# A hybrid SSD and attention layer: the decay products of the scan on VectorE instead of GpSimd, and two sets of attention logits in one step of the plan

## The chip, the cores and the metric

One core of a Trainium2 chip runs the whole layer as one program. The metric is the device time of one execution in microseconds. Engines are named as in the profile: PE (TensorE matmuls), PEld (TensorE weight loads), DVE (VectorE), ACT (ScalarE), POOL (GpSimd), SP (SyncE, which here only issues transfers).

## The reference

One layer of a streaming encoder, for a prompt of 1024 rows and eight running streams of 16 rows each, 1152 rows together. Each row is projected to 12336 columns; two mixers run on the result, a chunked state-space scan (32 heads in 8 groups) and an attention with forget gates (16 heads), and their gated sum is projected again and normalized.

```python
h = einsum('bld,de->ble', x, w_in)
z, xbc, dt_raw, q, k, v, f_raw, g_path, mg_m, mg_a = split_projection(h)
xbc = silu(causal_conv(xbc))                       # x, B and C columns
acum  = cumsum(dt * A)                             # per chunk and head
decay = exp(where(causal, acum[:, None] - acum[None], -inf))
m      = (C @ B^T) * decay * dt
y_diag = m @ x
y_off  = (C @ state) * exp(acum)                   # per chunk, state carried on
y = rmsnorm_groups((y_diag + y_off + d_skip * x) * silu(z)) * mnorm_w
s = q @ k^T / 8 + (c_q - c_k), masked;  o = softmax(s) @ v    # c: cumsum of log f
u = sigmoid(g_m) * (y @ w_br_m) + sigmoid(g_a) * ((o * silu(g_path)) @ w_br_a)
x_new = layer_norm(2**0.25 * x + u @ w_out)
```

The streams do the same with a cached state, and with 1024 cached keys and values ahead of their own 16 rows. Everything is float32.

## The kernel before, in words

Activations lie with columns on the partitions and the 1152 rows along the free axis, in three pieces (`c` = 0, 1, 2) of 384. A dense tile (`dense`) makes 128 output columns: for each piece 8 slices of the input times three products (L244, L245, L246; weights and activations are split into a high and a low part), 24 matmuls into one PSUM bank named `d`. There are two such banks, so a piece can begin when the piece before the last has been emptied by ACT and DVE. After every six dense matmuls the program calls `flow.tick()`, which may put a step of some other work, written as a generator, between them on PE.

In the scan stage the dense tiles of group g + 1 (in the order z0, x0, x1, z1, b, c) run beside the scan of group g. A convolved tile is emptied by ACT (L539, L540, and L545 for the streams' part of the third piece), then worked on by DVE (three L551), ACT (L552) and DVE (L553). A z tile takes ACT L569 and DVE L570. Each new weight tile is split by ACT (L223 or L226, `wh`) and then by POOL (L224) or DVE (L227, `wl`).

The scan of a group goes through the pieces c = 0, 1, 2, called its three blocks below. For each block `decay` makes, for four heads: `m`, the differences of the cumulative decays (DVE, L687, three instructions per head), the exponential of `ce` in place (ACT, L689), the exponential of `m` (ACT, L690), `m` times the causal C B^T (DVE, L691), and `ce` times C (L692), which stands in the matmul with the carried state (L712). `ce` is the row of cumulative decays, loaded from DRAM onto all partitions. POOL also gates the outputs (L724), adds their squares (L730), scales x by the weights (L614) and the state by its decay (L667).

In the scan stage a scheduler orders the instructions of each engine by their due times, so taking an instruction to another engine changes the order around it. From attention on the order is the one in which the code is written, under `tc.manual_schedule()`.

Attention runs per pair of heads (`pair`), beside the dense tiles of the next pair. Its steps stand in a table `plan`: a due time, a cost that is taken off the time to the next step, and the functions to call. A step whose time has come is called at the next tick. `scores(j, i)` makes the prompt's logits of query block j against key block i in a PSUM tile `s2` (two buffers), `least` and `mins` their row minima, and `s_scores(half)` the logits of four of the eight streams against their cached keys, in another `s2` buffer and a bank `y`.

Of the kernel before, what the change touches and what calls it, by code (L numbers as in the profile page):

```python
# [15 lines left out]
ALU = mybir.AluOpType  # L16
# [133 lines left out]
def trunk_step(ctx: ExitStack, tc: tile.TileContext, I, O):  # L150
    nc = tc.nc
    ve, ac, po, te, sy = nc.vector, nc.scalar, nc.gpsimd, nc.tensor, nc.sync
# [438 lines left out]
    def group(g, r):  # L591

        sp = lazy["spb"]
        xs, z, Bf, Cf = [r["x0"], r["x1"]], [r["z0"], r["z1"]], r["b"], r["c"]
# [84 lines left out]
        def decay(c, i):  # L679
            w = CW if c < 2 else 256  # L680
            for e in range(2):
                h = 4 * g + 2 * i + e
                m = sp.tile([P, 3, P], F32, tag="m", name=f"m{c}_{h}", bufs=4)
                ce = ces[c, 2 * i + e]
                for j in range(3):
                    b = 3 * c + j
                    ve.tensor_scalar(m[:, j, :], ce[:, j * P:(j + 1) * P], nacum[:, b, h:h + 1], 0.0,  # L687
                                     ALU.add, ALU.min)
                ac.activation(ce[:, :w], ce[:, :w], AF.Exp)  # L689
                ac.activation(m[:], m[:], AF.Exp)  # L690
                ve.tensor_tensor(m[:], m[:], cbms[c][:], ALU.mult)  # L691
                po.tensor_tensor(ce[:, :w], ce[:, :w], Cf[c][:, :w], ALU.mult)  # L692
                mm[c, 2 * i + e] = m

        def readout(c):
# [76 lines left out]
        for c in range(NCH):  # L772
            for j in range(3):
                transp(3 * c + j)
                yield Y
                if c and j == 0:
                    readout(c - 1)
                    yield 2 * Y
            cbt(c)
            yield Y  # L780
            if c == 2:
                stk = stack()
                sample_out()
                yield Y
            decay(c, 0)
            yield Y
            states(c)
            if c == 2:
                for q in range(4):
                    sample_decay(q)  # L790
            yield Y
            decay(c, 1)
            if c < 2:
                for i in range(2):
                    rows(c + 1, i)
            yield Y
# [80 lines left out]
    def pair(hp, r):  # L877
# [227 lines left out]
        def last(i):  # L1105
# [32 lines left out]
            (45.7, 4.4, (values, 2), (scores, 1, 0), (scores, 1, 1), (least, 1, 0)),  # L1138
            (46.0, 0.0, (load, "v", hp, 1, 0)),
            (49.4, 0.0, (least, 1, 1), (mins, 1, 1, "a")),  # L1140
            (53.8, 0.8, (scores, 0, 0)),
            (54.6, 0.0, (least, 0, 0), (mins, 0, 0, "a")),
            (55.4, 2.6, (s_scores, 1)),
            (62.2, 0.2, (share, "a", (0, 1))),
            (62.4, 0.0, (s_weights, 1)),
            (62.8, 0.0, (load, "v", hp, 1, 1)),
# [64 lines left out]
    with tc.manual_schedule():  # L1211
        r = keys(0, r)
        for hp in range(1, 8):
            flow.start(pair(hp - 1, r))
            gate_dense(GATES_SSD + hp - 1, fp, "kv1", 3)
            r = keys(hp, q_and_gate(hp))
        flow.start(pair(7, r))
        for j in range(GATES_SSD + 7, GATES_SSD + 7 + GATES_FOX):
            gate_dense(j, fp, "kv1", 3)
        flow.drain()  # L1220
# [139 lines left out]
    for c in range(NCH):  # L1360
# [27 lines left out]
        for j in range(3):  # L1388
            b, w = 3 * c + j, width[j]
# [107 lines left out]
```

## Time and profile before

| | |
|---|---|
| median of 3 runs | 2066.13 us (2064.82 to 2066.86) |
| the profiled execution | 2064.78 us |
| its span | 2062.9 us, 36057 instructions |
| granted TensorE clock | 0.999 of full speed |
| scan with its dense tiles | about 190 to 1000 us, some 100 us per group |
| attention with its dense tiles | about 1000 to 1650 us |
| branch and output projections | the rest |

A row of the stretches view gives the stretch, its length, then busy time and number of instructions of PE, PEld, DVE, ACT and POOL, the granted clock, the share of the DMA engines and GB/s. A row of the groups view gives line, engine, operation, output and inputs, shapes and count, then busy time and mean ns of one, then the idle time of the engine ahead of them and what ended it. A row of the waits view names the waiting engine and line, what it waited for, the sum in us, how often, and the longest. A row of a timeline gives start and duration in us, the instruction, how many were merged, and in brackets the idle time of the engine ahead of it with what ended that. Matmuls are pipelined: the distance of two starts is what one costs.

### The profile page before, as it was taken

What the parts mean: (1) busy time and instruction counts of PE and PEld (TensorE: products, weight loads), DVE (VectorE), ACT (ScalarE), POOL (GpSimd) and SP (SyncE); (2) the same over time, 40 slices, a digit from 0 to 9 for tenths busy, and PEclk for the clock granted to TensorE, in tenths of its full rate; (3) what the DMA queues carried; (4) which work ended last, traced back from release to release, by engine and by line L of the source; (5) the groups of instructions that cost most, each with busy time, mean ns of one, the idle gap of its engine ahead of it and who ended that gap; (6) DMA issues with size and microseconds to landing.
All of it is one profiled execution on the core that took longest, in us unless ns stands there. A gap on an engine that the chain in (4) does not pass through costs nothing.

```text
span 2062.9 us, 36057 instructions
## 1 busy us (share of the span) xinstructions
PE 2028.5 (98%) x14263; PEld 1868.2 (91%) x14263; DVE 1376.8 (67%) x2278; ACT 820.1 (40%) x1647; POOL 594.6 (29%) x775
## 2 busy tenths in 40 slices
PE   9999999999999999999999999999999999999998
PEld 7899989899998999999988888888889899999987
DVE  4145788887878787874487787777777774173355
ACT  5124444444434344443445554545455452122210
POOL 0013565555556564644100100110010002114400
PEclk9999999999999999999999999999999999999999
DMA  6412242423232323242556566556656584154222
GB/s 221 161 65 90 71 134 71 126 77 119 81 126 78 118 91 114 87 134 91 185 196 194 186 206 207 188 179 199 212 184 202 186 301 147 41 171 152 82 106 92
DMA packets 123624, 292.49 MB, mean 142 GB/s; under 512 B 18632, under 2 KB 74944, under 8 KB 113216
## 3 DMA queue, kind: packets, MB, share of 16 engines
q1 hardware_dynamic: 110912, 208.93, 31.7%
q10 hardware_dynamic: 12544, 81.27, 11.4%
q8 instruction: 112, 1.84, 0.4%
q14 instruction: 56, 0.46, 0.1%
HBM read 233.64 MB, written 56.51 MB: 141 GB/s over the span
## 4 chain that ended last, share of the span: by engine, by line
PE 67%; DVE 20%; ACT 5%; DMA 4%; issue 2%; POOL 1%; ACTq 0%; DVEq 0%; SPq 0%; POOLq 0%
PE d L244 14%; PE d L246 13%; PE d L245 13%; PE s L914 3%; DVE m L687 2%; PE o L989 2%; PE v L333 2%; PE v L334 2%; PE v L332 2%; PE dq L245 2%; PE dq L244 2%; PE dq L246 2%; PE out L1381 2%; PE out L1380 2%; PE out L1382 2%
## 5 line engine op out<-in xcount | busy, mean ns | idle before, releaser
L244 PE MATMUL d<-xh,wh 128*128 128x384 f32 x2112 | 740.9, 351 | 21.3 <-DVE z3z L570 2.1
L246 PE MATMUL d<-xh,wl 128*128 128x384 f32 x2112 | 708.7, 336 | 0.0
L245 PE MATMUL d<-xl,wh 128*128 128x384 f32 x2112 | 707.8, 335 | 0.0
L244 PEld LDWEIGHTS d<-xh,wh 128*128 128x128 f32 x2112 | 397.2, 188 | 54.6 <-issue 17.7
L245 PEld LDWEIGHTS d<-xl,wh 128*128 128x128 f32 x2112 | 397.6, 188 | 0.8
L246 PEld LDWEIGHTS d<-xh,wl 128*128 128x128 f32 x2112 | 396.7, 188 | 0.0
L224 POOL TENSOR_TENSOR wl<-wr,wh 128x1024 fp32r<-128x1024 f32 x52 | 125.5, 2413 | 348.8 <-ACT wh L223 348.8
L687 DVE TENSOR_SCALAR m<-ce,nacum 128x128 f32<-128x128 f32 x288 | 141.6, 553 | 5.9 <-PE y L708 5.9
L223 ACT CAST wh<-wr 128x1024 fp32r<-128x1024 f32 x64 | 67.0, 1047 | 194.9 <-PE d L245 157.1
L919 ACT ACTIVATE st<-s,ckt 128x256 f32<-128x256 f32 (+1 forms) x320 | 115.1, 466 | 20.1 <-PE s L914 14.8
L923 POOL TENSOR_TENSOR st<-st,mask_bf 128x256 f32<-128x256 f32 x64 | 48.3, 775 | 196.8 <-ACT st L919 196.7
L979 ACT ACTIVATE st<-st 128x1024 f32<-128x1024 f32 x80 | 83.1, 1062 | 43.6 <-DVE st L974 41.0
L227 DVE SCALAR_TENSOR_TENSOR wl<-wr,wh 128x1024 fp32r<-128x1024 f32 x50 | 62.2, 1243 | 32.5 <-ACT wh L226 32.1
L614 POOL TENSOR_TENSOR wx<-xdt,wdt 128x256 f32<-128x256 f32 x72 | 56.8, 790 | 50.9 <-DVE xdt L612 50.9
L989 PE MATMUL o<-st,vt 128*64 128x256 f32 (+1 forms) x640 | 69.5, 363 | 1.6 <-ACT st L979 1.2
L989 PEld LDWEIGHTS o<-st,vt 128*64 128x64 f32 x640 | 42.8, 137 | 28.4 <-ACT st L979 5.1
L245 PE MATMUL d<-yb1l,wh 128*128 128x384 f32 x192 | 64.2, 334 | 0.0
L244 PE MATMUL d<-yb1h,wh 128*128 128x384 f32 x192 | 64.2, 334 | 0.0
L246 PE MATMUL d<-yb0h,wl 128*128 128x384 f32 x192 | 64.2, 334 | 0.0
L246 PE MATMUL d<-yb1h,wl 128*128 128x384 f32 x192 | 64.2, 334 | 0.0
L245 PE MATMUL d<-yb0l,wh 128*128 128x384 f32 x192 | 64.2, 334 | 0.0
L244 PE MATMUL d<-yb0h,wh 128*128 128x384 f32 x192 | 64.2, 334 | 0.0
(635 smaller groups left out, 4093.9 us busy)
## 6 DMA issues: line engine op xcount, KB each, us to landing
wr<-in_wt SPq DMA_DIRECT2D x88, 512.0 KB
kc<-in_cache_k ACTq DMA_DIRECT2D x32, 1024.0 KB
vc<-in_cache_v ACTq DMA_DIRECT2D x32, 1024.0 KB
ce<-ac_d SPq DMA_DIRECT2D x96, 192.0 KB
wr<-in_wbr SPq DMA_DIRECT2D x24, 512.0 KB
gate_d<-gate SPq DMA_DIRECT2D x48, 192.0 KB
sb<-cs_d ACTq DMA_DIRECT2D x16, 576.0 KB
yr<-ym_d SPq DMA_DIRECT2D x16, 576.0 KB
```

The source lines that it names most:

```text
L223: ac.copy(hi[:, :cols], raw[:, :cols])
L224: lazy.get("sub", po).tensor_tensor(lo[:, :cols], raw[:, :cols], hi[:, :cols].bitcast(F32), ALU.subtract)
L227: ve.scalar_tensor_tensor(lo[:, :cols], raw[:, :cols], scale, hi[:, :cols].bitcast(F32), ALU.mult, ALU.subtract)
L244: te.matmul(out, wh, xh, start=(k == 0), stop=False)
L245: te.matmul(out, wh, xl, start=False, stop=False)
L246: te.matmul(out, wl, xh, start=False, stop=(k == n - 1))
L614: po.tensor_tensor(wx[b][:], xdt[b][:], wdt[:, b, hs][:, :, None].to_broadcast([P, 4, 64]), ALU.mult)
L687: ve.tensor_scalar(m[:, j, :], ce[:, j * P:(j + 1) * P], nacum[:, b, h:h + 1], 0.0, ALU.add, ALU.min)
L914: te.matmul(ps2[:, e, 256 * x + q0:256 * x + 256], kk[hr, ks], qq[hr, qs], start=(at == 0), stop=(at == 2))
L919: ac.activation(S[j][:, e, kb, q0:], ps2[:, e, 256 * x + q0:256 * x + 256], AF.Identity, bias=ckt[:, kb, 2 * hp + e:2 * hp + e + 1])
L979: ac.activation(w, w, AF.Exp, scale=-1.0)
L989: te.matmul(o[64 * e:64 * e + 64, 256 * at + q0:256 * at + 256], vt[:, kb, 64 * e:64 * e + 64], S[j][:, e, kb, q0:256], start=(kb == 0), s ...
```

## The change

There are two edits. The product of `ce` with C is issued on DVE instead of POOL, 96 instructions in all (8 groups, 3 blocks, 4 heads). And in the plan of a head pair the block 0 logits with their minima and the streams' second logits, three steps before, are one step with the sum of their costs.

```diff
@@ decay(c, i), in the scan
                 ac.activation(ce[:, :w], ce[:, :w], AF.Exp)
                 ac.activation(m[:], m[:], AF.Exp)
                 ve.tensor_tensor(m[:], m[:], cbms[c][:], ALU.mult)
-                po.tensor_tensor(ce[:, :w], ce[:, :w], Cf[c][:, :w], ALU.mult)
+                ve.tensor_tensor(ce[:, :w], ce[:, :w], Cf[c][:, :w], ALU.mult)
                 mm[c, 2 * i + e] = m
@@ plan, in pair(hp, r)
             (49.4, 0.0, (least, 1, 1), (mins, 1, 1, "a")),
-            (53.8, 0.8, (scores, 0, 0)),
-            (54.6, 0.0, (least, 0, 0), (mins, 0, 0, "a")),
-            (55.4, 2.6, (s_scores, 1)),
+            (53.8, 3.4, (scores, 0, 0), (least, 0, 0), (mins, 0, 0, "a"), (s_scores, 1)),
             (62.2, 0.2, (share, "a", (0, 1))),
```

What the first edit does to the order is seen at the second block of a group, here the scan of group 3 (heads 12 to 15) beside the tiles `acc4x` and `raw4x` of group 4. On DVE before: the last differences `m`, three L551 on the second piece of an x tile, and what follows.

```order
L687 TENSOR_SCALAR m_14_5481<-ce_14_5190,nacum 128x128 x3
L687 TENSOR_SCALAR m_15_5489<-ce_15_5192,nacum 128x128 x3
L551 SCALAR_TENSOR_TENSOR acc4x_1_5279<-raw4x_1_5278,cw,acc4x_1_5279 128x384 x3
L553 SCALAR_TENSOR_TENSOR acc4x_1_5279<-raw4x_1_5278,acc4x_1_5279 128x384
L612 TENSOR_TENSOR xdt_4_5334<-tp_4_5330,dtm 128x256
L227 SCALAR_TENSOR_TENSOR wl_5341<-wr_5136,wh_5340 128x1024
```

DVE now, in the same place:

```order
L687 TENSOR_SCALAR m_15_5489<-ce_15_5192,nacum 128x128 x3
L551 SCALAR_TENSOR_TENSOR acc4x_1_5279<-raw4x_1_5278,cw,acc4x_1_5279 128x384
L692 TENSOR_TENSOR ce_13_5188<-ce_13_5188,acc3c_4911 128x384
L551 SCALAR_TENSOR_TENSOR acc4x_1_5279<-raw4x_1_5278,cw,acc4x_1_5279 128x384
L692 TENSOR_TENSOR ce_14_5190<-ce_14_5190,acc3c_4911 128x384
L551 SCALAR_TENSOR_TENSOR acc4x_1_5279<-raw4x_1_5278,cw,acc4x_1_5279 128x384
L692 TENSOR_TENSOR ce_15_5192<-ce_15_5192,acc3c_4911 128x384
L612 TENSOR_TENSOR xdt_4_5334<-tp_4_5330,dtm 128x256
L227 SCALAR_TENSOR_TENSOR wl_5341<-wr_5136,wh_5340 128x1024
L553 SCALAR_TENSOR_TENSOR acc4x_1_5279<-raw4x_1_5278,acc4x_1_5279 128x384
```

Three products stand between and behind the L551 (the fourth, of head 12, stands a few rows ahead), and L553 has moved behind the weight split.

ACT in the same place, as one piece of the difference (- before, + now):

```order
 L689 ACTIVATE ce_15_5192<-ce_15_5192 128x384
 L690 ACTIVATE m_15_5489<-m_15_5489 128x384
+L226 ACTIVATE wh_5340<-wr_5136 128x1024
 L552 ACTIVATE raw4x_1_5278<-acc4x_1_5279 128x384
-L226 ACTIVATE wh_5340<-wr_5136 128x1024
 L539 COPY raw4x_2_5313<-d_2_5288 128x256
 L540 ACTIVATE acc4x_2_5314<-d_2_5288,cb,cw 128x384
```

The weight split now stands ahead of the tanh L552 that needs DVE's L551, and so no longer between it and the evacuation of the third piece.

In the scan PE has the same rows in the same order as before. In attention, PE at the block 0 logits of the first pair (`s_0_0`), before:

```order
L914 MATMUL s_0_0_11034<-qh_10011,kh_10363 128x128 x2
L914 MATMUL s_0_0_11034<-ql_10012,kh_10363 128x128 x2
L914 MATMUL s_0_0_11034<-qh_10011,kl_10364 128x128 x2
L244 MATMUL d_1_11026<-xh_92,wh_10684 128x384
L245 MATMUL d_1_11026<-xl_93,wh_10684 128x384
L246 MATMUL d_1_11026<-xh_92,wl_10685 128x384
```

and now:

```order
L914 MATMUL s_0_0_11034<-qh_10011,kh_10363 128x128 x2
L914 MATMUL s_0_0_11034<-ql_10012,kh_10363 128x128 x2
L914 MATMUL s_0_0_11034<-qh_10011,kl_10364 128x128 x2
L1038 LDWEIGHTS ident_bf
L1038 MATMUL sn_1_11062<-mask_bf,ident_bf 32x128
```

The streams' second logits (`sn_1`, `ss_1`) follow at once; before, six dense matmuls stood between. It is so in all eight pairs. DVE and POOL keep their order there.

## The prediction

> **What bounds the kernel now.** I read the busy times first, then stretches of the span, then what PE waits for, then the timelines of DVE, ACT and POOL around those waits.
>
> ```profile
> PE 2028.5 (98%) x14263; PEld 1868.2 (91%) x14263; DVE 1376.8 (67%) x2278; ACT 820.1 (40%) x1647; POOL 594.6 (29%) x775
> ...
> 470.00:570.00 100.00, 96.83 (x658) 91.35 (x657) 81.58 (x150) 43.11 (x94) 57.08 (x77) 1.00 0.31 101
> ...
> 1200.00:1300.00 100.00, 100.00 (x949) 86.56 (x944) 75.61 (x105) 51.38 (x101) 11.18 (x20) 1.00 0.63 204
> ```
>
> PE is the bound at full clock (1.00). The two stretches are one scan group and a piece of attention: in the scan PE is idle 3 us in 100, in attention not at all. So edit 1 (the products) can win only PE's idle time in the scan, and edit 2 (the logits) only the cost of changing between kinds of matmul. Idle PE time over the scan (190 to 1000 us), first the group that carries it, then the waits, first and last of each kind:
>
> ```profile
> L244 PE MATMUL d<-xh,wh 128*128 128x384 f32 x1183 | 415.9, 352 | 21.3 <-DVE z3z L570 2.1 <-DVE z6z L570 1.8 <-DVE z2z L570 1.8
> ...
> PE d L244 <- DVE z3z L570: 2.1, 2, 1.6
> ...
> PE d L244 <- DVE z4z L570: 1.8, 2, 1.5
> PE d L244 <- ACT raw1x L545: 1.0, 1, 1.0
> ...
> PE d L244 <- ACT raw2x L545: 1.0, 1, 1.0
> ...
> PE d L244 <- ACT raw4c L545: 0.4, 1, 0.4
> PE d L244 <- ACT raw3c L545: 0.4, 1, 0.4
> ```
>
> Seven z waits make 2.1 + 6 x 1.8 = 12.9 us, seven x waits 7.0, two c waits 0.8: 20.7 of the 21.3. In each the next dense chunk wants a PSUM bank `d` that ACT or DVE has not emptied. The question is whether edit 1 makes the emptying earlier or later.
>
> **Edit 1: 96 products move from POOL to DVE.** First what they cost where they are: the first block of heads in one group, on DVE and POOL.
>
> ```profile
> L692 POOL TENSOR_TENSOR ce<-ce,acc3c 128x384 f32<-128x384 f32 (+1 forms) x12 | 12.0, 1009 | 9.2 <-DVE acc3c L553 5.0 <-ACT ce L689 4.2
> ...
> 494.13 1.26 DVE L687 TENSOR_SCALAR m<-ce,nacum 128x128 f32<-128x128 f32 x2
> 495.31 4.10 DVE L551 SCALAR_TENSOR_TENSOR acc3c<-raw3c,cw,acc3c 128x384 f32<-128x384 f32 x3
> ...
> 494.30 1.99 POOL L692 TENSOR_TENSOR ce<-ce,acc3c 128x384 f32<-128x384 f32 x2 [5.00 <-DVE acc3c L553]
> ...
> 497.71 1.28 POOL L692 TENSOR_TENSOR ce<-ce,acc3c 128x384 f32<-128x384 f32 x1
> ...
> 554.79 0.48 DVE L687 TENSOR_SCALAR m<-ce,nacum 128x128 f32<-128x128 f32 x2
> ...
> 540.01 0.62 DVE L551 SCALAR_TENSOR_TENSOR acc4x<-raw4x,cw,acc4x 128x384 f32<-128x384 f32 x1
> 540.54 0.55 DVE L691 TENSOR_TENSOR m<-m,cbm 128x384 f32<-128x384 f32 x1
> 541.01 0.61 DVE L551 SCALAR_TENSOR_TENSOR acc4x<-raw4x,cw,acc4x 128x384 f32<-128x384 f32 x1
> ```
>
> With POOL idle (the last four rows) two L687 take 0.48 us, an L551 takes 540.54 - 540.01 = 0.53 of DVE's time and an L691, a product of two SBUF tiles of the moved shape, 541.01 - 540.54 = 0.47. Beside L692 two L687 take 1.26 and three L551 4.10: DVE loses 0.78 + (4.10 - 1.59) = 3.3 us to four products, 0.8 each. Such DVE work gets through about once per POOL instruction.
>
> The price of one moved product is therefore bounded by the cost 0.47 less a relief up to 1.0 (a mean L692 is 1009 ns): -0.53 to +0.47 us, and up to +1.4 if it is itself caught behind a POOL product that stays (L724, L730, about 1 us each). I take -0.35 (0.47 - 0.8), since these rows show exactly this work; here it makes 4 x -0.35 = -1.4 us. A 256-wide product (third block) I take as 0.34 us, an estimate between L687 and L691 by width.
>
> The x wait, second block of heads, on DVE, POOL, ACT and PE:
>
> ```profile
> 526.13 3.79 DVE L687 TENSOR_SCALAR m<-ce,nacum 128x128 f32<-128x128 f32 x7
> 529.84 3.18 DVE L551 SCALAR_TENSOR_TENSOR acc4x<-raw4x,cw,acc4x 128x384 f32<-128x384 f32 x3
> ...
> 526.29 1.01 POOL L724 TENSOR_TENSOR z3z<-z3z,yt 128x384 f32<-128x384 f32 x1 [0.69 <-DVE yt L721]
> 527.26 1.01 POOL L692 TENSOR_TENSOR ce<-ce,acc3c 128x384 f32<-128x384 f32 x1
> 528.22 1.02 POOL L730 TENSOR_TENSOR sqs<-sqs,yt 128x384 f32<-128x384 f32 x1
> ...
> 529.97 2.63 POOL L692 TENSOR_TENSOR ce<-ce,acc3c 128x384 f32<-128x384 f32 x2 [0.56 <-ACT ce L689]
> ...
> 533.11 0.53 ACT L552 ACTIVATE raw4x<-acc4x 128x384 f32<-128x384 f32 x1 [1.98 <-DVE acc4x L551]
> 533.54 1.04 ACT L226 ACTIVATE wh<-wr 128x1024 fp32r<-128x1024 f32 x1
> 535.31 0.27 ACT L545 COPY raw4x<-d 128x128 f32<-128x128 f32 x1
> ...
> 535.62 0.45 PE L244 MATMUL d<-xh,wh 128*128 128x384 f32 x1 [1.02 <-ACT raw4x L545]
> ```
>
> PE wants the bank at 534.6 (535.62 - 1.02). Before it is free, DVE must finish three L551 (533.0), then ACT does L552, L226 (1.04) and the evacuation, ending 535.58. Relief up to there: the three L551 lose 3.18 - 1.59 = 1.6 us to two L692, the pair before them, one of which stands at 527.26, 0.8 each as above, together 3.2. The new code puts three products ahead of or between them (the fourth stands behind): 3 x 0.47 = 1.4. The L551 end about 1.8 earlier, at 531.2. In the new order ACT also does L226 ahead of L552, while DVE still works, which takes its 1.04 off the chain: the bank is free near 535.6 - 1.8 - 0.8 = 533.0, before 534.6. All of the x wait goes: -7.0 us. If the relief were absent, L226's move alone would bring it 0.8 earlier and the products 1.4 later.
>
> The z wait, third block of heads:
>
> ```profile
> 553.30 0.52 ACT L552 ACTIVATE raw4x<-acc4x 128x384 f32<-128x384 f32 x1 [3.93 <-DVE acc4x L551]
> ...
> 562.17 0.52 ACT L690 ACTIVATE m<-m 128x384 f32<-128x384 f32 x1 [0.61 <-DVE m L687]
> 562.60 0.47 ACT L569 ACTIVATE z4z<-d 128x384 f32<-128x384 f32 x1
> ...
> 558.48 3.60 DVE L687 TENSOR_SCALAR m<-ce,nacum 128x128 f32<-128x128 f32 x5
> ...
> 563.10 0.56 DVE L570 SCALAR_TENSOR_TENSOR z4z<-z4z,d 128x384 f32<-128x384 f32 x1 [0.69 <-ACT z4z L569]
> ...
> 563.71 0.44 PE L244 MATMUL d<-xh,wh 128*128 128x384 f32 x1 [1.54 <-DVE z4z L570]
> ```
>
> The z evacuation L569 is queued on ACT behind the last exponential, which waits for L687; five of them take 3.60 us instead of 5 x 0.2 + 0.1 = 1.1. L724 and L730 stay on POOL, so perhaps half of that is won back, and two products (0.7) now stand between the last L687 and L570 on DVE, each waiting for its own ACT exponential. Going through the new order by hand, the bank comes 0.7 us earlier from the same start (between 0 and 1.4). The start moves too: at 553.30 ACT had waited 3.93 us for DVE, so the chain into this block is paced by DVE and ACT, not by PE, and inherits some 2.5 us from the second block, of which PE takes back 1.0 since its x wait is gone. Together 0.7 + 1.5 = 2.2 against the 1.54 needed. Margin 0.7, error of about 1: I leave 0.35 per group, 7 x 0.35 = 2.5, and take 12.9 - 2.5 = 10.4.
>
> The c waits hang on the first block, 1.4 us earlier by the sum above: -0.8. Behind the moved products on DVE stand L551, L612 and L570, counted above; ACT's L552 and L569 wait for them. POOL loses 12.0 us per group, its products that stay come earlier; PE reads `ce` only a block later. On SP only one store and one load at the last group change places: 0.
>
> **Edit 2: the second logits follow block 0's at once.** The kernel already does one such pair adjacent (blocks of j = 2 and the first logits); rows of PE, first the adjacent, then the separated pair:
>
> ```profile
> 1103.97 0.34 PE L246 MATMUL d<-xh,wl 128*128 128x384 f32 x1
> ...
> 1107.47 0.34 PE L245 MATMUL d<-xl,wh 128*128 128x384 f32 x1
> ...
> 1134.87 0.34 PE L246 MATMUL d<-xh,wl 128*128 128x384 f32 x1
> ...
> 1139.62 0.34 PE L245 MATMUL d<-xl,wh 128*128 128x384 f32 x1
> 1139.79 0.33 PE L246 MATMUL d<-xh,wl 128*128 128x384 f32 x1
> ```
>
> From the last dense matmul ahead to the second one behind, the adjacent pair takes 1107.47 - 1103.97 = 3.50 us and the separated one 4.75, of which the six dense matmuls between are 6 x 0.17 = 1.02 (the last two rows give their spacing). The difference 0.23, by eight head pairs, is -1.8 us. The worst is that the second logits come before their PSUM buffer is empty, a wait bounded by the 1.02 that the dense matmuls used to cover: -1.8 to 8 x 1.02 = +8.2. I take -1.8, as the adjacent pair shows no wait.
>
> **Sum.** -7.0 - 10.4 - 0.8 - 1.8 = -20.0. The profiled execution took 2064.8 us (span 2062.9 and 1.9 around it), 1.4 under the median 2066.1; off the median, 2046.
>
> **Rivals.** A: the z wait stays. ACT waits in line for each product's exponential and DVE ends the third block no sooner. For it: the margin of 0.7 is small, and L724 and L730 stay. Against: the head start. Then -7.0 - 0.8 - 1.8 = -9.6: 2056.5.
> B: no effect. The lock's loss only moves to POOL's remaining products (57 - 12 = 45 us of 100 stay there) and the waits keep their size: 2064 to 2066. Against: they come on no more DVE work than before.
> C: DVE becomes the bound, slower. Place: second and third block. If a moved product costs its 0.47 or 0.34 and half of them are caught behind a POOL product for 1 us, with no relief, the banks come 4 x 0.47 + 2 and 4 x 0.34 + 2, so 7 us per group, later: 7 x 7 = 49, less the 1.8: 2113. It decides as soon as the relief per product is under 0.47; the rows show 0.8. In favour, DVE is at 82% of the group. The Trainium skill ("Perfetto Trace Analysis", Optimizing Scalar/DVE Operations) says that with a saturated DVE it may make sense to hand work to another engine, GpSimd included, though with a port shared by those two it might not help; by its first half this change goes the wrong way and C's time would come, by the second the rows above decide.
>
> **Chances.** Main case 0.56 (2042 to 2051), A 0.26 (2051 to 2061), B 0.09, C 0.09. Less than 0.2% (4 us) is about what a measurement of this kernel can't tell from no change. Faster 0.82, same 0.09, slower 0.09. The range runs from 2042 (all 21.3 and 1.8 gone, and 1 us of spread between runs) to 2060, leaving out B, C and A's end.
>
> **What the new profile would show.** Right: L687's mean falls from 553 toward 350 ns; the x and c waits are gone from PE's list and z is under 0.5 per group; PE's busy share in a scan group is over 99 in 100; DVE's busy time there is the same or lower. Edit 2: one pair 3.5 us instead of 4.75. Wrong: L692 on DVE takes over 0.9 us in the mean, PE waits for `z` longer than 1.8, or new waits on `y` from L692 appear.

## The result, and the profile after

The changed kernel takes 2035.49 us (median, 2034.88 to 2036.44), the kernel before on the same chip 2066.49: a ratio of 0.985, with a 95% interval of 0.9833 to 0.9867. That is 31 us less, where 20 were forecast; 2035.5 lies below the range that began at 2042. The direction and the mechanism held, the size did not.

From the page of the changed kernel, its busy times; then the same stretch of the scan as before; and the groups of the scan, 190 to 1000 us, that answer to those of the prediction:

```profile
PE 2019.1 (99%) x14263; PEld 1867.2 (92%) x14263; DVE 1356.3 (67%) x2374; ACT 818.1 (40%) x1647; POOL 508.3 (25%) x679
```

```profile
470.00:570.00 100.00, 100.00 (x685) 95.24 (x685) 83.03 (x170) 43.91 (x97) 48.26 (x67) 1.00 0.36 112
```

```profile
L244 PE MATMUL d<-xh,wh 128*128 128x384 f32 x1226 | 428.9, 350 | 0.0
...
L687 DVE TENSOR_SCALAR m<-ce,nacum 128x128 f32<-128x128 f32 x288 | 105.7, 421 | 5.9 <-PE y L708 5.9
...
L692 DVE TENSOR_TENSOR ce<-ce,acc2c 128x384 f32<-128x384 f32 x8 | 4.3, 550 | 0.1
...
L692 DVE TENSOR_TENSOR ce<-ce,acc2c 128x256 f32<-128x256 f32 x4 | 2.5, 629 | 0.0
```

PE is idle 0.0 in the stretch that had 3.2 us of idle time, and L244's idle column, 21.3 before, is 0.0. L687 falls from 553 to 421 ns. DVE, which took over 96 products, is busy 20 us less in the whole program (1356.3 against 1376.8). What PE waits for, the whole list:

```profile
PE o L989 <- ACT st L979: 2.0, 4, 0.6
PE sot L1075 <- DVE rowma L951: 1.8, 4, 0.8
PE warm L352 <- DVE pre L499: 1.2, 1, 1.2
PE s L914 <- ACT st L919: 1.0, 1, 1.0
PE ss L1042 <- ACT st L919: 0.2, 1, 0.2
```

None of the z, x and c waits is left. What is left belongs to the attention, but for the warm-up. The first logits of the attention (L914) show how far ahead the scan ends; first and last start, before and then after:

```profile
L914 PE MATMUL s<-qh,kh x320: 215/278/386, 1006.1 to 1616.5; 64*128 64x256 f32 x128, 64*128 64x128 f32 x32
```

```profile
L914 PE MATMUL s<-qh,kh x320: 215/278/386, 975.2 to 1586.5; 64*128 64x256 f32 x128, 64*128 64x128 f32 x32
```

1006.1 - 975.2 = 30.9 us are won by the first logits, 30.0 of them are left at the last. So the scan gave all of it, and the attention nothing that shows.

**Where 21.3 us of idle time became 31.** Here are the same four places of one group on PE's timeline, before:

```profile
501.67 0.27 PE L608 MATMUL tp<-ident,acc3b 128*128 128x128 f32 x1
502.32 0.44 PE L244 MATMUL d<-xh,wh 128*128 128x384 f32 x1 [0.38 <-ACT raw3c L545]
...
506.95 0.83 PE L643 MATMUL cb<-acc3c,acc3b 128*128 128x128 f32 x6
508.00 0.44 PE L244 MATMUL d<-xh,wh 128*128 128x384 f32 x1 [0.22 <-DVE z4z L570]
...
533.77 0.83 PE L643 MATMUL cb<-acc3c,acc3b 128*128 128x128 f32 x6
535.62 0.45 PE L244 MATMUL d<-xh,wh 128*128 128x384 f32 x1 [1.02 <-ACT raw4x L545]
...
561.83 0.34 PE L246 MATMUL d<-xh,wl 128*128 128x384 f32 x1
563.71 0.44 PE L244 MATMUL d<-xh,wh 128*128 128x384 f32 x1 [1.54 <-DVE z4z L570]
```

and after:

```profile
485.68 0.27 PE L608 MATMUL tp<-ident,acc3b 128*128 128x128 f32 x1
485.70 0.42 PE L244 MATMUL d<-xh,wh 128*128 128x384 f32 x1
...
493.74 0.83 PE L643 MATMUL cb<-acc3c,acc3b 128*128 128x128 f32 x6
494.33 0.42 PE L244 MATMUL d<-xh,wh 128*128 128x384 f32 x1
...
520.05 0.83 PE L643 MATMUL cb<-acc3c,acc3b 128*128 128x128 f32 x6
520.64 0.42 PE L244 MATMUL d<-xh,wh 128*128 128x384 f32 x1
...
546.65 0.34 PE L246 MATMUL d<-xh,wl 128*128 128x384 f32 x1
546.82 0.43 PE L244 MATMUL d<-xh,wh 128*128 128x384 f32 x1
```

The reader should compare starts, not the figures in brackets. From L608 to L244 it was 0.65 and is 0.02: 0.63 us, listed as 0.38. From L643 to L244 in the first block 1.05 against 0.59: 0.46, listed as 0.22. In the second block 1.85 against 0.59: 1.26, listed as 1.02. In the third 1.88 against 0.17: 1.71, listed as 1.54. A matmul's row lasts 0.33 us and the next starts 0.17 later, so the row's modelled end covers the first 0.17 to 0.25 us of every stall, and a stall shorter than that isn't listed at all. Taken matmul by matmul over the 6293 matmuls up to the first logits (PE's order is the same in both), the lead grows at the L643-L244 steps by 12.5 us (3.7 in first blocks, 8.8 in second), at the z step by 12.0, at the L608-L244 steps by 3.3, just behind stalls by 0.8 and at one transpose by 0.8, together 29.4. The other 1.5 us are spread over many small steps.

### The profile page after: what moved, and what is told of

It is laid out like the page before. It is cut to its first block, busy times and chain, and to the rows that moved or that the text cites. A ratio compares the mean times of both kernels' runs of the same rounds, so it can differ in the third digit from the quotient of the medians.

```text
span 2033.0 us, 36030 instructions
## 1 busy us (share of the span) xinstructions
PE 2019.1 (99%) x14263; PEld 1867.2 (92%) x14263; DVE 1356.3 (67%) x2374; ACT 818.1 (40%) x1647; POOL 508.3 (25%) x679
## 4 chain that ended last, share of the span: by engine, by line
PE 90%; DVE 4%; DMA 3%; ACT 1%; issue 1%; POOL 0%; SPq 0%; ACTq 0%; DVEq 0%
PE d L244 21%; PE d L246 20%; PE d L245 20%; PE s L914 3%; PE o L989 2%; PE y L708 2%; PE dq L245 2%; PE dq L246 2%; PE dq L244 2%; PE out L1380 2%; PE out L1378 2%; PE out L1379 2%; PE v L333 2%; PE v L334 2%; PE v L332 2%; DVE st L974 1%
## 5 line engine op out<-in xcount | busy, mean ns | idle before, releaser
L244 PE MATMUL d<-xh,wh 128*128 128x384 f32 x2112 | 737.8, 349 | 0.0
L244 PEld LDWEIGHTS d<-xh,wh 128*128 128x128 f32 x2112 | 397.0, 188 | 25.4 <-issue 16.7
L687 DVE TENSOR_SCALAR m<-ce,nacum 128x128 f32<-128x128 f32 x288 | 105.7, 421 | 5.9 <-PE y L708 5.9
L227 DVE SCALAR_TENSOR_TENSOR wl<-wr,wh 128x1024 fp32r<-128x1024 f32 x50 | 62.0, 1239 | 30.8 <-ACT wh L226 30.8
L989 PE MATMUL o<-st,vt 128*64 128x256 f32 (+1 forms) x640 | 69.8, 364 | 2.4 <-ACT st L979 2.0
L989 PEld LDWEIGHTS o<-st,vt 128*64 128x64 f32 x640 | 42.8, 137 | 29.7 <-ACT st L979 6.6
L689 ACT ACTIVATE ce<-ce 128x384 f32<-128x384 f32 (+1 forms) x96 | 46.5, 484 | 44.8 <-DVE m L687 44.4
L244 PE MATMUL d<-yb0h,wh 128*128 128x384 f32 x192 | 64.2, 334 | 0.0
L244 PE MATMUL d<-yb1h,wh 128*128 128x384 f32 x192 | 64.2, 334 | 0.0
```

What stands on the lines that cost most here:

```text
L227: ve.scalar_tensor_tensor(lo[:, :cols], raw[:, :cols], scale, hi[:, :cols].bitcast(F32), ALU.mult, ALU.subtract)
L244: te.matmul(out, wh, xh, start=(k == 0), stop=False)
L989: te.matmul(o[64 * e:64 * e + 64, 256 * at + q0:256 * at + 256], vt[:, kb, 64 * e:64 * e + 64], S[j][:, e, kb, q0:256], start=(kb == 0), s ...
```

## The experiments

"Before" is the kernel before, measured beside each on the same chip.

| kernel | us | before | ratio, 95% interval |
|---|---|---|---|
| edit 1 alone | 2034.71 | 2064.82 | 0.9857 (0.9844 to 0.9870) |
| edit 2 alone | 2065.49 | 2064.82 | 1.0002 (0.9993 to 1.0011) |
| with POOL's squares | 2069.17 | 2064.82 | 1.0019 (1.0010 to 1.0028) |
| with DVE paid twice | 2059.99 | 2064.82 | 0.9976 (0.9967 to 0.9986) |
| product left out | 2033.39 | 2066.08 | 0.9841 (0.9824 to 0.9857) |
| first block only | 2058.09 | 2066.08 | 0.9959 (0.9944 to 0.9974) |
| second block only | 2048.08 | 2066.08 | 0.9911 (0.9896 to 0.9926) |
| third block only | 2061.57 | 2066.08 | 0.9980 (0.9970 to 0.9989) |
| logits set apart | 2049.28 | 2067.11 | 0.9916 (0.9902 to 0.9931) |
| with POOL's copies | 2046.78 | 2067.11 | 0.9903 (0.9886 to 0.9919) |
| two steps later | 2049.38 | 2065.91 | 0.9922 (0.9902 to 0.9941) |
| changed kernel again | 2033.92 | 2065.91 | 0.9846 (0.9834 to 0.9859) |

### Each edit alone

Edit 1 alone has the changed L692 and the old plan:

```diff
-                po.tensor_tensor(ce[:, :w], ce[:, :w], Cf[c][:, :w], ALU.mult)
+                ve.tensor_tensor(ce[:, :w], ce[:, :w], Cf[c][:, :w], ALU.mult)
```

> Edit 1 alone: the 96 products of L692 on DVE, the attention's order of before. If edit 2 is worth its -1.8 us in the changed kernel, this one takes 2035.5 + 1.8 = 2037.3 us; if what the adjacent logits save is lost again in new stalls of the attention, 2035.5 +/- 0.5. By both theories of edit 1 nearly the whole gain of 31 us is here, and the first attention matmul comes some 30 us earlier in the program than before. If less than 25 us of the gain were here, the two edits would work together, which no theory says.

Edit 2 alone has the old L692 and the changed plan:

```diff
-            (53.8, 0.8, (scores, 0, 0)),
-            (54.6, 0.0, (least, 0, 0), (mins, 0, 0, "a")),
-            (55.4, 2.6, (s_scores, 1)),
+            (53.8, 3.4, (scores, 0, 0), (least, 0, 0), (mins, 0, 0, "a"), (s_scores, 1)),
```

> Edit 2 alone: the logits in one go, the products on POOL as before. Worth -1.8 us: 2064.7. Lost again in the stalls at L989 and L1075: 2066.5, with the stage from the first streams' matmul to the last as long as before within 0.7 us. A loss of over 1 us (2067.5 or more) would be a third reading: the adjacent logits cost by themselves, and edit 1 hides it.

Edit 1 alone gives 30.1 us of the 31. Edit 2 alone gives +0.7 us, by its interval -1.4 to +2.3: its -1.8 isn't there, though less of it may be. Its rows do what was forecast; here they are on PE in the changed kernel, from the last dense matmul ahead of the pair to the second one behind:

```profile
1102.96 0.34 PE L246 MATMUL d<-xh,wl 128*128 128x384 f32 x1
...
1106.46 0.34 PE L245 MATMUL d<-xl,wh 128*128 128x384 f32 x1
```

That is 3.50 us, the number predicted, so 0.23 per pair are won between kinds of matmul. But the attention has stalls of its own, which vary. The two that carry them, first in edit 1 alone and then in edit 2 alone:

```profile
PE o L989 <- ACT st L979: 2.3, 6, 0.6
PE sot L1075 <- DVE rowma L951: 2.1, 4, 0.9
```

```profile
PE sot L1075 <- DVE rowma L951: 1.6, 3, 0.8
...
PE o L989 <- ACT st L979: 1.5, 4, 0.6
```

They make 4.4 and 3.1 us here, 2.1 in the kernel before and 3.8 in the changed one. They differ between kernels whose attention is the same (edit 1 alone and before), so a term of 1.8 is below what one execution tells.

### Is it POOL that holds DVE up?

Behind DVE's product stands a POOL instruction of the same shape, so POOL keeps the number of its instructions:

```diff
+                po.tensor_tensor(ce[:, :w], ce[:, :w], ce[:, :w], ALU.mult)
```

> The changed kernel, and behind each product on DVE a POOL instruction of the same shape that squares ce in place (other values come out; the number of instructions on POOL and their time are as before). It tells the relief of DVE from the mere change of engine. Theory T (DVE and POOL hold each other up: what was won is the 0.8 us that DVE loses beside each of POOL's products): DVE now has the 0.47 us of its own product and the 0.8 us lost as well, x and z waits come back at least as long as before, 2066 or more, up to 2066 + 41 (96 products by 0.43 us of cost, if DVE sets the pace). Rival O (the gain is from the order of ACT, L226 ahead of L552, and from products that no longer wait across engines): the POOL squares cost nothing, 2036 to 2040.

```profile
PE d L244 <- DVE z1z L570: 2.0, 2, 1.5
...
PE d L244 <- ACT acc1x L540: 1.4, 1, 1.4
```

```profile
L687 DVE TENSOR_SCALAR m<-ce,nacum 128x128 f32<-128x128 f32 x288 | 126.4, 493 | 6.1 <-PE y L709 6.0 <-DMA ce<-ac_d 0.2
...
L693 POOL TENSOR_TENSOR ce<-ce 128x384 f32<-128x384 f32 (+1 forms) x96 | 88.7, 934 | 43.8 <-DVE ce L692 42.9 <-DMA ym_d<-z5z 0.9
```

It takes 2069.2: the whole gain is gone and 4 us more. The z and x waits are back on PE's list, and L687 is at 493 ns. The order of ACT (L226 ahead of L552) is that of the changed kernel, and so is DVE's, so the order isn't where the gain came from; rival O falls. Theory T's lower end is met: DVE pays for its products and is still held up.

The second form asks whether a POOL instruction with one input does the same:

```diff
+                po.tensor_copy(ce[:, :w], ce[:, :w])
```

> Like the kernel with POOL's squares, but POOL copies ce onto itself (one input instead of two; the values stay). It tells which POOL instructions hold DVE up. If any POOL instruction on these tiles does: 2062 to 2070, with L687's mean near the 493 ns of the kernel with the squares. If it takes an instruction with two inputs: L687 near 421 ns as in the changed kernel, PE's waits gone, 2035 to 2038.

```profile
PE d L244 <- DVE z2z L570: 1.2, 1, 1.2
```

```profile
L687 DVE TENSOR_SCALAR m<-ce,nacum 128x128 f32<-128x128 f32 x288 | 116.2, 457 | 6.0 <-PE y L709 6.0
...
L693 POOL COPY ce<-ce 128x384 f32<-128x384 f32 (+1 forms) x96 | 61.0, 650 | 42.6 <-DVE ce L692 40.2 <-DMA ym_d<-z1z 1.1 <-DMA ym_d<-z0z 0.7
```

Neither number came: 2046.8, in between. A copy does hold DVE up (L687 457 ns against 421), but it lasts 650 ns where a square lasts 934, and PE's z waits come back at 1.0 to 1.2 us each, the x waits at 0.2. The shorter POOL instruction costs less; whether by its length or by its single input these two kernels don't tell apart. The Trainium skill ("SBUF — State Buffer", Who interferes with whom) says that DVE and GpSimd share one pair of ports, which one of them holds for a whole instruction while the other waits, and that a DVE instruction with two inputs contends with any GpSimd instruction that reads SBUF. The copies agree: DVE's L227, which has two inputs, takes 1289 ns in the mean of the scan with them, against 1233 in the changed kernel, so one input on POOL's side is enough.

### How much slack DVE has left

Behind each product a second DVE instruction that leaves the values as they are:

```diff
+                ve.tensor_tensor(ce[:, :w], ce[:, :w], ce[:, :w], ALU.max)
```

> The changed kernel, and behind each product on DVE a second DVE instruction of the same shape (the maximum of ce with itself, so the values stay): the price of the moved work is paid twice, 96 x about 0.43 = 41 us more of DVE time, 12 per group, POOL as in the changed kernel. If DVE has slack in the scan (82% busy by the windows of before, about 620 of 810 us after): PE's waits come back in part only, 2036 to 2045. If the changed kernel stands just at the edge of its slack (rival C's mechanism, only not yet reached): x and z waits come back, 3 to 6 us per group, 2055 to 2080.

```profile
PE d L244 <- DVE z5z L570: 2.6, 2, 2.3
```

It takes 2060.0, 24.5 us above the changed kernel, which is within the second reading; but only the z waits are back, seven of 2.3 us, and x and c waits are not on the list. DVE is busy 37.5 us longer in the whole program (1393.8 against 1356.3). From start to start the seven z steps are 17.1 us longer than in the changed kernel, and 6.3 us more come just behind them: after four of the seven stalls the granted clock was one half for 3.4 us, and dense matmuls stood 0.32 us apart in place of 0.17. The stretches view of one of the four:

```profile
461.50:464.80 3.30, 3.30 (x13) 3.30 (x13) 0.97 (x3) 2.01 (x4) 2.31 (x4) 0.50 0.06 22
```

The kernel before, whose z steps took 1.9 us where these take 2.6, had no such stretch in its scan. Why four stalls brought one and three did not is open. So less of DVE's added work reaches PE as waits than the time suggests. The changed kernel stands at the edge in the third block and has room in the second. Its own rows say so, on ACT and DVE ahead of the two places shown above:

```profile
518.93 0.27 ACT L545 COPY raw4x<-d 128x128 f32<-128x128 f32 x1
...
546.20 0.56 DVE L570 SCALAR_TENSOR_TENSOR z4z<-z4z,d 128x384 f32<-128x384 f32 x1
```

In the second block the bank is free at 519.20 and PE wants it at 520.64, 1.4 us later. In the third it is free at 546.76 and PE goes on at 546.82. Where PE did wait there, before, it started 0.05 us behind the same end (563.10 + 0.56 to 563.71), so next to nothing is to spare.

The other way round, L692 is left out altogether:

```diff
-                po.tensor_tensor(ce[:, :w], ce[:, :w], Cf[c][:, :w], ALU.mult)
```

> The changed kernel without L692 at all: ce is not multiplied by C (other values come out), 96 instructions fewer and nothing in their place. It asks whether anything of edit 1's cost is left in the time. If PE is the only bound of the scan in the changed kernel (no idle PE time left there): 2035.5 +/- 1, the moved products cost nothing. If DVE still holds PE up in gaps too short for the list of waits: lower, by up to 8 groups x 0.5 = 4 us, 2031 to 2033.

Its 2033.4 us lie between the two readings, but its interval, 0.9824 to 0.9857, holds the changed kernel's 0.985, and the first logits start at the same time, within what the stages ahead vary:

```profile
L913 PE MATMUL s<-qh,kh x320: 215/278/385, 974.9 to 1585.0; 64*128 64x256 f32 x128, 64*128 64x128 f32 x32
```

974.9 against 975.2: the products on DVE cost nothing that shows, and PE alone sets the scan.

This kernel also tells the relief from the order. Without L692 the instructions of DVE and PE up to the attention stand in the order of the kernel before, and ACT's too, but for one L690 in each group; L226 comes behind L552, as it did before:

```profile
516.74 0.53 ACT L552 ACTIVATE raw4x<-acc4x 128x384 f32<-128x384 f32 x1 [0.18 <-DVE acc4x L551]
517.17 1.05 ACT L226 ACTIVATE wh<-wr 128x1024 fp32r<-128x1024 f32 x1
```

The whole gain is there all the same (1006.1 to 974.9), so ACT's new order isn't needed for it.

### One block at a time

Only one block's products go to DVE (c == 0, 1 or 2), with edit 2:

```diff
+                (ve if c == 0 else po).tensor_tensor(ce[:, :w], ce[:, :w], Cf[c][:, :w], ALU.mult)
```

> Edit 2, and of edit 1 only the first block of heads (c = 0, 4 products of each group) on DVE. By the starts of PE's matmuls in the two traces this block's own gaps (c 0.5 and the C transposes 0.4 us per group) are 0.9 x 7 = 6 us. Each wait has its own cause: -6 us, 2060. The chain is handed on (the prediction's working: 1.4 us of head start, which the x wait of 1.26 inherits): -6 - 9 = -15, 2051. Neither (the relief is taken by POOL's products of the next block): 2065.

> Edit 2, and of edit 1 only the second block (c = 1) on DVE. Each wait has its own cause: the x wait alone goes, 7 x 1.26 = -9 us, 2057. Handed on: the third block starts 1.5 us earlier as well, and the z wait of 1.70 goes down to about 0.2, -9 - 10.5 = -19, 2047. Neither: 2065.

> Edit 2, and of edit 1 only the third block (c = 2) on DVE. The prediction's working: from the same start the bank comes 0.7 us earlier, 7 x 0.7 = -5 us, 2061, with a z wait of about 1.0 left and x and c waits as before. If the third block's products alone make the whole z wait: 7 x 1.70 = -12, 2054. If the z wait hangs on the head start alone: 2065.

First logits (first start) and PE's waits, in the order first, second and third block:

```profile
PE d L244 <- DVE z3z L570: 1.6, 1, 1.6
...
PE d L244 <- ACT raw6x L545: 1.1, 1, 1.1
```

```profile
L914 PE MATMUL s<-qh,kh x320: 215/278/385, 999.0 to 1610.2; 64*128 64x256 f32 x128, 64*128 64x128 f32 x32
```

```profile
PE d L244 <- DVE z3z L570: 1.1, 2, 0.5
```

```profile
L914 PE MATMUL s<-qh,kh x320: 215/278/385, 988.9 to 1597.8; 64*128 64x256 f32 x128, 64*128 64x128 f32 x32
```

```profile
PE d L244 <- DVE z2z L570: 1.1, 2, 0.9
```

```profile
L914 PE MATMUL s<-qh,kh x320: 215/278/385, 1002.1 to 1615.5; 64*128 64x256 f32 x128, 64*128 64x128 f32 x32
```

The first logits come 7.1, 17.2 and 4.0 us earlier, and the times fall by 8.0, 18.0 and 4.5, together 30.5. At the scan's start (190 us) these executions were already 1.4, 0.3 and 1.1 us behind the kernel before, so the scan itself wins 8.5, 17.4 and 5.0, together 30.9, where the changed kernel's scan wins 30.8. The first block takes away its own gaps (3.6 at L643, 3.3 at L608, 0.8 at a transpose) and leaves the x waits at 1.0 to 1.1: nothing is handed on to them. The prediction's lines had only 0.8 us of it as c waits; of the rest, 2.0 us were booked as the second, small one of each "z, 2 times" (now "1"), and the others were too short for the list or hidden behind the modelled ends. The second block takes the x waits and is handed on: of the 1.71 us of each z gap, 1.0 go. The third block takes the other 0.71 (7 x 0.71 = 5.0), the number that the prediction had for it from the same start.

### What a change between kinds of matmul costs

The opposite of edit 2, in the changed kernel's plan; the first of five places:

```diff
-            (0.0, 2.6, (scores, 3, 0), (scores, 3, 1), (least, 3, 0)),
-            (3.2, 0.2, (last, 0)),
+            (0.0, 1.3, (scores, 3, 0)),
+            (1.9, 1.3, (scores, 3, 1), (least, 3, 0)),
+            (3.4, 0.2, (last, 0)),
...
```

> The changed kernel with the opposite of edit 2, six times in each head pair: logits that follow each other at once, or follow the values at once, are set apart by some dense matmuls (five places, six more changes between kinds of matmul; the same matmuls in all). The price of one separation by edit 2's rows is 0.225 us (1.80 by 8). If that price counts in full: 6 x 8 x 0.225 = +10.8 us, 2046. If changing between kinds of matmul is hidden by stalls that the stage has anyway (the reading that edit 2 is worth nothing): 2035.5 to 2038. Under 2035 if the separated logits come with fewer stalls for DVE's and ACT's results than the adjacent ones.

The time rises by 13.8 us against the changed kernel's first median; the intervals of the two ratios don't touch. Changing kinds is paid in full, and more. In the trace five more logits a head pair stand behind a dense matmul, one fewer than meant, so 40 separations. The stage from the first L914 to the last L1064 is 13.3 us longer. PE's waits in it only changed places:

```profile
PE d L244 <- DVE kl L862: 5.3, 7, 1.3
```

This one is new and stands alone; the 5.0 of the changed kernel (L989, L1075, L914, L1042) are gone. So some 13 us come from 40 separations, 0.33 each, above the 0.225 of edit 2's pair.

That the stalls vanished when PE came to these places later suggested a version to try:

```diff
-            (63.8, 0.2, (sums, 2), (s_out, 0)),
-            (66.4, 1.2, (turn_s, 1)),
+            (63.8, 0.0, (sums, 2)),
+            (65.4, 0.2, (s_out, 0)),
+            (66.8, 1.2, (turn_s, 1)),
...
-            (74.8, 7.4, (values, 0, 1), (sums, 1), (s_values, 1, 0), (s_values, 1, 1), (sums, 0), (s_norm, 1), (load, "k", hp + 1, 0, 1)),
+            (75.8, 7.4, (values, 0, 1), (sums, 1), (s_values, 1, 0), (s_values, 1, 1), (sums, 0), (s_norm, 1), (load, "k", hp + 1, 0, 1)),
```

> The changed kernel with two steps of the attention's order put later by about one unit: the streams' output (s_out, L1075) from 63.8 to 65.4 and the last values (L989) from 74.8 to 75.8, dense matmuls taking their places. If the stalls that eat edit 2's saving are PE coming too early at these two places: the waits at L1075 and L989 (3.8 us together in the changed kernel's list) go to under 1, and the time falls by 2 to 4 us against the changed kernel on the same chip, 2032 to 2033.5. If the waits only follow (they hang on ACT's exponentials and DVE's reductions, which come later too): 2035.5 as the changed kernel.

> The changed kernel itself, beside the run with two later steps on the same chip. A second profile of it shows how far the stalls of the attention differ between two executions of one program. Both readings expect 2035.5 +/- 1; the one that puts edit 2's saving below what single profiles tell expects the list's waits at L1075 and L989 to come out differently from the first profile's 3.8 us, by 1 us or more.

Both readings of the later steps were wrong. The waits at L1075 and L989 are gone, as the first said, but the time is 2049.4 (its runs from 2042 to 2056), 15 us above the changed kernel beside it. A new wait has come, first here and then what the changed kernel's second profile shows:

```profile
PE d L244 <- DVE kl L862: 17.8, 7, 4.1
```

```profile
PE sot L1075 <- DVE rowma L951: 1.4, 2, 0.8
...
PE o L989 <- ACT st L979: 1.0, 3, 0.6
```

In seven pairs PE wants a bank that DVE's L862, the rounding of the next pair's keys, has not emptied. Why it is late stays open. The profiled execution also had a clock of 0.993, against 0.999 in the changed kernel: behind the four longest of the seven waits the granted clock was one half for 3.4 to 6.8 us. The runs spread with it, from 2042 us at 0.998 to 2056 at 0.993. In the second profile of the changed kernel the two waits make 2.4 us, not 3.8: the spread of 1 us or more that was expected.

## Why the prediction was wrong

**The mechanism held.** L692's cost was taken as 0.47 us and its relief as 0.8, and DVE's net time fell, by 20.5 us or 0.21 for each product, where -0.35 was taken. All of the x wait went, as forecast: the bank was to be free 2.6 us earlier in relation to PE (535.6 to 533.0). It was 1.2 late and is 1.4 early. L687 went to 421 ns ("toward 350"), PE's share in the group to 100 of 100, and no wait on `y` came from L692. Of the two causes named, the POOL instructions are shown from both sides: with as many of them as before the gain is gone, though ACT's new order stays, and without L692 the gain is whole, though ACT's order is the old one. So the 0.8 us that the prediction gave to L226's move was not needed; what the new order adds by itself wasn't measured.

**The first step that failed is the first paragraph's: edit 1 "can win only PE's idle time in the scan", read as 21.3 us.** That column counts from modelled ends. Measured from start to start the gaps were 29.4 us. The terms:

| term | forecast | measured in starts |
|---|---|---|
| x waits | -7.0 | -8.8 |
| z waits | -10.4 | -12.0 |
| c waits, with L608's gaps | -0.8 | -7.0 |
| behind stalls, one transpose | none | -1.6 |
| edit 2 | -1.8 | +0.7 (-1.4 to +2.3), in time |

The c term was the worst, 0.8 for 7. The prediction summed what the list called c and didn't ask what the second "time" of each z row was: some 0.25 us at the first block's L643, 2.0 in all. Like with like, it put the first block at 2.8 us for 7.0 and the z step at 8.4 for 12.0. The range's low end, 2042, was built from the same column ("all 21.3 and 1.8 gone"), so it failed with it.

**The second is the 2.5 us left on the z wait.** The margin was given as 0.7 with an error of about 1. By the blocks the parts were 0.71 from the block's own products (forecast 0.7) and 1.0 handed on (forecast 1.5): just enough for the 1.71, with next to nothing to spare. So the deduction for a possible remainder was paid for nothing. It was no safe call: the kernel with DVE paid twice shows how close it lies.

**The third is edit 2.** The price between kinds of matmul was right in the rows (3.50 us), but an effect of 1.8 us doesn't come out of stalls that vary by some 2 us between executions. The prediction's own bounds for it, -1.8 to +8.2, hold zero, but the sum took their lower end.

**The rivals.** A (z stays) and B (no effect) fall with the lists. C's mechanism, DVE as the bound, is real but one step further on: with the products paid twice the time rises by 24.5 us, 17.1 of it in the z steps. What the prediction said decides it, the relief per product under its cost, is what the POOL squares made true, and there the kernel was slower than before by 4 us, where C's price was 49 less 1.8. The half of the products that C has caught for 1 us each were not: on DVE they took 0.55 to 0.63 us in the mean.

## What to carry to other kernels

Size the idle time of a pipelined engine from the starts of its instructions, at a stall and at the same place without one; a list of waits gives the places, but here it held about seven tenths of the time. Where DVE is slow beside a busy POOL, moving POOL's work onto DVE can free more DVE time than it costs, which a comparison of the same instruction beside POOL and alone tells beforehand. And before a term of 1 or 2 us is added to a sum, look how far the stalls of that stage differ between two executions.

## What was not expected of the hardware

- POOL's copies with one input hold DVE's work up as well (L687 457 ns against 421), only for less time than its products of two inputs (493 ns).
- The relief isn't spread evenly: moving the second block's products alone gave 18.0 us, more than the first and third together (8.0 + 4.5), since it is handed on to the third block.
- Setting logits apart costs 0.33 us for each separation, more than the 0.23 that edit 2's pair shows.
- Behind some stalls PE also ran slow: with the products paid twice, four of seven z steps of 2.6 us were followed by 3.4 us at a granted clock of one half, which cost some 1.6 us each. None followed the 1.9 us steps of the kernel before.
